# A four-layer hybrid encoder on one core: stacked gate logits, lower weight parts by adding DMAs, and other orders at three places

## The chip, the cores and the metric

The kernel runs on one core of a Trainium2 chip. The core has a matrix engine (TensorE, PE in the rows), a vector engine (DVE), an activation engine (ACT), a general engine (GpSimd, POOL) and a queue engine (SyncE, SP). Each works through its own instructions in order, and semaphores join them. The metric is the device time of one execution in microseconds (us).

## The reference, cut to what matters

Four layers work on 512 tokens of 1024 features: retention, a conformer convolution, gated linear attention (GLA) and retention again, each followed by an MLP with a squared ReLU. The GLA mixer makes a gate from a low-rank product, and normalises each head before a silu gate:

```
def log_gate(d):
    logits = (u @ gate_w1[d]) @ gate_w2[d] + gate_b[d]
    return split_heads(jax.nn.log_sigmoid(logits.astype(F32)) / GLA_GATE_NORMALIZER, GLA_HEADS)

o = bidirectional_scan(q, k, v, log_gate(0), log_gate(1))
o = merge_heads(rmsnorm(o, norm_gain)) * jax.nn.silu(r)
return o @ w_out
```

The gate's rank is 16. Retention rotates q and k by angles made of the positions, which needs a sine and a cosine of large arguments. The convolution has 31 taps over time for each feature, then a layer norm, a silu and a product.

## The kernel before

All activations lie with features on the partitions: a tile is 128 features by 512 tokens. Every fp32 product is made of three matmuls of rounded parts: high by high, low by high, high by low (`mm3`, lines 454 to 456). A weight panel is 128x1024. `Stream.prep` loads it into one of three raw buffers (`wraw`, a DMA on SP's queue), ACT copies it into the high part `whi` (line 146), and DVE subtracts to get the low part `wlo` (line 147). The ring holds six such pairs.

TensorE's order is the order in which the code is written. Norms and other side work are put into that order by `after(us, fn)`: the function runs when the matmuls written since then add up to so many us (`tick`). On ACT and DVE a scheduler orders the work by its own idea of time, except in blocks under `manual_schedule`, where the written order holds: the first norm (ACT, DVE), the convolution's taps and layer norm (ACT, DVE), and GLA (ACT). POOL is written by hand in layer 0.

The places that matter are these.

- The start. `first_norm` loads `h` and the first panels and splits `h` into `xh` and `xl`. `norm_sums` squares `h` on ACT (line 266) in halves of 256 tokens, and DVE adds the squares up (line 267). The mean of squares is a matmul (line 285), which `norm_at = 22.0` puts 22 us behind the start of the projections. `angles` (line 746) makes the sine and cosine: ACT rounds the angle to `ahi` (line 757), POOL takes off multiples of whole turns by five rounds of products (lines 772 to 779), DVE finishes (lines 762 to 789), ACT takes the sine, and `sr` and `cr` go out to HBM. DVE then rotates q and k (lines 865 to 867) and splits them into `qkh` and `qkl` (line 442). The first scores read those.
- The convolution. Tokens go in two halves, c0 and c1. `stats` takes mean and variance and the reciprocal root, with a load of ACT's table ahead of it (line 1192) and another behind it (line 1195). `finish` makes the silu (line 1206) and the split `zh`, `zl` of each of eight tiles. `second` (line 1235) runs `stats(c1)`, then tile 7 of c0, then the rest of c1.
- GLA. The gate's inner product leaves `u1`, split into `ogh` and `ogl`. `logits` makes eight `mm3` from it. For each head, `scores` copies a PSUM bank to `tmp` (line 1431), overwrites a block (line 1432), and splits it. `attend` makes the output, and `gate` a silu gate (lines 1525 and 1526). In the last head one gate lies ahead of `attend` and one behind it, and `fin` places the norm's mean.

In what follows, panel n of GLA is the one that lies n behind the stream's position (`W.at`) where the layer begins, as the diff counts them: panel 9 holds k's weights of head 1, panel 15 the second half of head 0's output weights.

Of the kernel before, what the change touches and what calls it, by code (L numbers as in the profile page):

```python
# [10 lines left out]
F32 = mybir.dt.float32  # L11
# [11 lines left out]
P = 128  # L23
# [5 lines left out]
HEADS = 4  # L29
CW = 31  # L30
PAD = CW // 2
TP = T + 2 * PAD
# [63 lines left out]
class Stream:  # L96


    def __init__(self, K, src, ahead):
        self.K, self.src, self.ahead = K, src, ahead  # L100
        self.n = src.shape[0]
        self.ready, self.loaded, self.at = [], 0, 0
        self.deep = 5
        self.aside = {}
        self.cut = {}
        self.pairs, self.steps = {}, []
        self.between = {}

# [4 lines left out]
    def prep(self, parts=1):  # L113

        if self.steps:
            self.steps.pop(0)()
            return []
        if self.loaded >= self.n:
            return []
        K = self.K  # L120
        nc = K.nc
        i = self.loaded
        if self.between.get(i):
            self.whole(self.between[i].pop(0), self.ring)
            return []
        if i in self.pairs:
            self.pair(i)
            return []
        self.loaded += 1
        if i in self.cut:  # L130
            self.whole(self.cut[i], self.aside.pop(i, self.ring))
            return []
        raw = K.wp.tile([P, 8 * P], F32, name="wraw", tag="wraw", bufs=3)
        hi, lo = self.aside.pop(i, self.ring)()
        pan = Panel(hi, lo)
        self.ready.append(pan)

        def load(a, b):
            nc.sync.dma_start(raw[:, a:b], self.src[i][:, a:b])

        def split(a, b):
            for c in range(a, b, min(pan.w, b - a)):
                d = c + min(pan.w, b - a)
                t, o = divmod(c, pan.w)
                h, l = (x[t][:, o:o + d - c] for x in (hi, lo))
                nc.scalar.activation(h, raw[:, c:d], AF.Copy)  # L146
                nc.vector.tensor_tensor(l, raw[:, c:d], h.bitcast(F32), ALU.subtract)  # L147

        if parts == 1:
            load(0, 8 * P)  # L150
            split(0, 8 * P)
        else:
            w = 8 * P // parts
            return [(lambda a=a: load(a, a + w), lambda a=a: split(a, a + w)) for a in range(0, 8 * P, w)]
# [188 lines left out]
class Kern:  # L343
# [166 lines left out]
    def norm_sums(self):  # L510

        self.hsum = Sums(self, D)
        for a, b in HALVES:
            for k in range(KD):
                self.hsum.add(self.h[k][:, a:b], (a, b))

    def norm(self, us, then):

        if self.hsum is None:
            self.norm_sums()  # L520
# [513 lines left out]
    def conv(self, layer, close):  # L1034
        nc = self.nc
        with self.tc.tile_pool(name="conv", bufs=1) as op:
            Z = [self.pair(op, "z", 2 * KD) for _ in range(KD)]
            with self.tc.tile_pool(name="taps", bufs=1) as cp:
# [148 lines left out]
                def stats(c):  # L1187
# [4 lines left out]
                    nc.scalar.preload_act_table_set("abs_reciprocal_sqrt_and_small")  # L1192
# [23 lines left out]
                with self.tc.manual_schedule(engines={ACT, DVE}):  # L1216
                    taps(c0)

                    def first():
                        complete(c0)  # L1220
                        stats(c0)
                        norm(c0)
                        finish(c0, 0, 1, 2, 3)
# [11 lines left out]
                    def second():  # L1235
                        stats(c1)
                        finish(c0, 7)
# [10 lines left out]
            with self.tc.tile_pool(name="outw", bufs=1) as wp:  # L1248
# [8 lines left out]
    def gla(self, layer, close):  # L1257
# [3 lines left out]
        with self.tc.tile_pool(name="gla", bufs=1) as gp:  # L1261
# [18 lines left out]

            u1 = self.pair(gp, "og", 8)
# [15 lines left out]
            def first(i, ps, c):  # L1297
                if i == 0:
                    t = self.tmp()
                    nc.vector.tensor_tensor(t[:, c[0]:c[1]], ps[:, c[0]:c[1]], self.r[:, c[0]:c[1]], ALU.mult)  # L1300
                    self.split(u1, t[:, c[0]:c[1]], c)
# [6 lines left out]

            def logits(p, h):
                for d in range(2):  # L1310
                    ps = self.ps()
                    self.mm3(ps, p.blk(d * HEADS + h), u1, True, True)
# [98 lines left out]
            def scores(h):  # L1411
# [7 lines left out]
                pr = []  # L1419
                for s in range(NB):  # L1420
# [12 lines left out]
                    p = self.pair(gp, "og", 8) if (h, s) == (0, 3) else self.pair(gp, "p" if s < 2 else "c23" if h + 1 == HEADS else "c01", 4)  # L1433
                    self.split(p, t)
                    pr.append(p)
# [29 lines left out]
            def attend(h, v, pr, g):  # L1465
# [22 lines left out]

                def finish():
                    self.rsqrt(ro, s2.mean((0, T)))  # L1490
                    if not g or h == 0:
                        for f in range(2):
                            normed(f)
                            if h == 0:
                                split(f)
# [3 lines left out]
                def rest():  # L1499
                    for f in range(len(g), 2):  # L1500
                        nc.vector.tensor_tensor(o[f], o[f], gate(), ALU.mult)
                        if not g:
                            split(f)
                    if h > 0 and g:
                        self.flush()
                        for f in range(2):
                            normed(f)
                            split(f)
# [39 lines left out]
            with self.tc.manual_schedule(engines={ACT}):  # L1548
                self.lead(3, first, tokens, 7.0)
                v = values(0)  # L1550
                p = self.W.next()
                logits(p, 0)
# [10 lines left out]
                for h in range(HEADS):  # L1563
# [16 lines left out]
                    if h > 0:  # L1580
                        g = [gate()] if last else []
                    rest = attend(h, v, pr, g)
# [13 lines left out]
    def run(self):  # L1596
        self.taps = [(0, 12), (8, 12), (8, 10), (8, 10), (8, 10), (16, 8), (24, 7), (16, 4)]
        self.shift_at = 40.0
        self.side = 6
        self.fin = 2.0, 7.0, 7.0, 2.0  # L1600
        self.ends = HALVES
        self.norm_at, self.tok_at = 22.0, 4.5
# [63 lines left out]
def _gla_panels(w_in, w1, w2, w_out):  # L1666
# [4 lines left out]
    for d in range(2):  # L1671
        w1p[:, 32 * d:32 * d + R] = w1[d]
        w2p[32 * d:32 * d + R, d] = w2[d]
# [84 lines left out]
```

## Time and profile before

| | us |
|---|---|
| three runs | 2712.33, 2715.22, 2720.29 |
| median | 2715.22 |
| the profiled execution | 2716.44 |
| its span in the trace | 2714.6 |
| TensorE busy | 2673.8 (98%) |
| DVE busy | 1934.6 (71%) |
| ACT busy | 1348.3 (50%) |
| POOL busy | 184.9 (7%) |

The engines' busy times add up to far more than the span because they overlap. TensorE's busy time lies 40.8 us under the span. The granted clock is shown for each window as a share of the full 2.4 GHz; a window that holds a stretch at 1.2 GHz shows a mean between 0.5 and 1. In a timeline a number in brackets is the time that the engine stood idle ahead of the instruction, with the instruction that released it.

### The profile page before, as it was taken

The page shows a single profiled execution, that of the slowest core. Times are in us where ns is not written, and L with a number is a line of the kernel's source. Part 1 is how long each engine was busy: PE and PEld are TensorE (multiplying, and loading weights), DVE is VectorE, ACT ScalarE, POOL GpSimd, SP SyncE. Part 2 cuts the span into 40 slices and gives each one's busy share as a digit, 9 for nine tenths or more (in the row PEclk, how much of TensorE's full clock was granted, in tenths as well). Part 3 has the DMA queues.
Part 4 walks back from the last instruction along what each step waited for, and adds up shares of the span by engine and source line. Part 5 has one row for each costly group of instructions (what it writes and reads, how often), then busy time and mean ns, then how long its engine had stood idle before and what let it go on. Part 6 is the DMA issues. An engine that isn't in the chain of part 4 may idle for free.

```text
span 2714.6 us, 38438 instructions
## 1 busy us (share of the span) xinstructions
PE 2673.8 (98%) x15238; PEld 2355.0 (87%) x15238; DVE 1934.6 (71%) x3016; ACT 1348.3 (50%) x2098; POOL 184.9 (7%) x207
## 2 busy tenths in 40 slices
PE   9999999999999999999999999999999999999998
PEld 7888889889998898999987888899888888989997
DVE  7755568877859977766788686677765555777766
ACT  5443444655536455554476555455544443555432
POOL 5420000000008400000000000000000000000000
PEclk9999999999999999999999999999999999999999
DMA  5433232776635422332222231333213222223322
GB/s 189 171 129 101 71 100 85 242 258 235 220 127 213 168 93 86 109 117 73 84 70 78 78 109 63 109 109 116 86 62 94 86 70 87 85 86 109 117 63 70
DMA packets 89028, 313.36 MB, mean 115 GB/s; under 512 B 9872, under 2 KB 12176, under 8 KB 88848
## 3 DMA queue, kind: packets, MB, share of 16 engines
q1 hardware_dynamic: 85536, 299.31, 33.4%
q0 software_dynamic: 3168, 11.54, 1.1%
q8 instruction: 119, 1.95, 0.3%
q14 instruction: 61, 0.50, 0.1%
q10 hardware_dynamic: 144, 0.07, 0.0%
HBM read 271.55 MB, written 39.32 MB: 115 GB/s over the span
## 4 chain that ended last, share of the span: by engine, by line
PE 82%; DVE 11%; ACT 3%; DMA 2%; POOL 1%; issue 1%; SPq 0%; DVEq 0%; ACTq 0%
PE ps L455 27%; PE ps L456 27%; PE ps L454 27%; DVE ps L1104 2%; DVE wlo L147 1%; DMA wraw<-in_wst_dram 1%; DMA cuth<-whi 1%; DVE acc L267 1%; ACT whi L146 1%; DVE tmp L329 1%; DMA cutl<-wlo 0%; DVE h L332 0%; PE st L275 0%; DVE actl L442 0%; DVE hc L1063 0%
## 5 line engine op out<-in xcount | busy, mean ns | idle before, releaser
L454 PE MATMUL ps<-xh,whi 128*128 128x256 f32 (+1 forms) x1920 | 644.0, 335 | 0.9 <-ACT xh L437 0.9
L455 PE MATMUL ps<-xl,whi 128*128 128x256 f32 (+1 forms) x1920 | 640.8, 334 | 1.1 <-DVE xl L444 1.1
L456 PE MATMUL ps<-xh,wlo 128*128 128x256 f32 (+1 forms) x1920 | 640.5, 334 | 0.0
L146 ACT ACTIVATE whi<-wraw 128x1024 fp32r<-128x1024 f32 (+1 forms) x300 | 312.2, 1045 | 317.5 <-PE ps L455 217.5
L147 DVE TENSOR_TENSOR wlo<-wraw,whi 128x1024 fp32r<-128x1024 f32 (+1 forms) x300 | 363.8, 1216 | 110.5 <-ACT whi L146 108.3
L455 PEld LDWEIGHTS ps<-xl,whi 128*128 128x128 f32 x1920 | 365.7, 190 | 38.7 <-DVE xl L444 1.5
L454 PEld LDWEIGHTS ps<-xh,whi 128*128 128x128 f32 x1920 | 365.9, 191 | 38.0 <-ACT xh L437 1.1
L456 PEld LDWEIGHTS ps<-xh,wlo 128*128 128x128 f32 x1920 | 365.8, 191 | 36.1 <-DVE wlo L147 0.5
L455 PE MATMUL ps<-actl,whi 128*128 128x512 f32 x896 | 350.1, 391 | 3.8 <-DVE actl L442 3.7
L454 PE MATMUL ps<-acth,whi 128*128 128x512 f32 x896 | 349.0, 390 | 0.6 <-ACT acth L435 0.6
L456 PE MATMUL ps<-acth,wlo 128*128 128x512 f32 x896 | 348.7, 389 | 0.0
L308 DVE TENSOR_TENSOR y<-y,ps 128x512 f32<-128x512 f32 (+1 forms) x200 | 114.8, 579 | 209.7 <-PE ps L456 209.0
L454 PE MATMUL ps<-wS,whi 128*128 128x256 f32 x768 | 217.7, 284 | 1.1 <-ACT tmp L654 1.1
L455 PE MATMUL ps<-wS,whi 128*128 128x256 f32 x768 | 217.3, 283 | 0.0
L456 PE MATMUL ps<-wS,wlo 128*128 128x256 f32 x768 | 217.3, 283 | 0.0
L455 PEld LDWEIGHTS ps<-actl,whi 128*128 128x128 f32 x896 | 168.2, 188 | 43.0 <-DVE actl L442 8.7
L454 PEld LDWEIGHTS ps<-acth,whi 128*128 128x128 f32 x896 | 168.2, 188 | 36.0 <-ACT acth L435 1.5
L456 PEld LDWEIGHTS ps<-acth,wlo 128*128 128x128 f32 x896 | 168.2, 188 | 34.6
L190 ACT ACTIVATE whi<-wraw 128x1024 fp32r<-128x1024 f32 x96 | 101.5, 1057 | 145.6 <-PE ps L455 114.8
L190 ACT ACTIVATE whi<-raw 128x1024 fp32r<-128x1024 f32 x96 | 81.2, 846 | 159.4 <-PE ps L455 126.3
L267 DVE TENSOR_TENSOR acc<-acc,sq 128x256 f32<-128x256 f32 (+1 forms) x246 | 121.3, 496 | 51.2 <-ACT sq L266 45.3
L454 PEld LDWEIGHTS ps<-wS,whi 128*128 128x128 f32 x768 | 147.4, 192 | 1.8 <-ACT tmp L654 1.7
(349 smaller groups left out, 5256.8 us busy)
## 6 DMA issues: line engine op xcount, KB each, us to landing
wraw<-in_wst_dram SPq DMA_DIRECT2D x390, 512.0 KB, 3.7
raw<-in_wst_dram SPq DMA_DIRECT2D x48, 512.0 KB, 4.2
cuth<-whi SPq DMA_DIRECT2D x24, 512.0 KB, 3.6
cutl<-wlo SPq DMA_DIRECT2D x24, 512.0 KB, 3.8
whi<-cuth SPq DMA_DIRECT2D x20, 512.0 KB, 3.3
wlo<-cutl SPq DMA_DIRECT2D x20, 512.0 KB, 4.3
diagh<-dg POOLq DMA_DIRECT2D x11, 512.0 KB, 3.2
diagl<-dg POOLq DMA_DIRECT2D x11, 512.0 KB, 3.2
```

What stands on the lines that cost most here:

```text
L146: nc.scalar.activation(h, raw[:, c:d], AF.Copy)
L147: nc.vector.tensor_tensor(l, raw[:, c:d], h.bitcast(F32), ALU.subtract)
L190: nc.scalar.activation(hi[0][:, :w], raw[:, :w], AF.Copy)
L267: nc.vector.tensor_tensor(acc, acc, t, ALU.add)
L308: self.K.nc.vector.tensor_tensor(y, y, ps[:, a:b], ALU.add)
L329: nc.vector.scalar_tensor_tensor(ts[k][:, a:b], self.ys[k][:, a:b], K.gain(self.layer, self.which, k), self.r[:, a:b], ALU.mult, ALU.mult)
L454: mm(out, lhsT=A[0], rhs=B[0], start=start, stop=False)
L455: mm(out, lhsT=A[0], rhs=B[1], start=False, stop=False)
L456: mm(out, lhsT=A[1], rhs=B[0], start=False, stop=stop)
L1104: nc.vector.scalar_tensor_tensor(sums[i], x, w, sums[i], ALU.mult, ALU.add)
```

## The change

Four parts of the code change.

1. The start. `norm_sums` takes its pieces as an argument, and the first norm (like the norms ahead of the convolution and GLA) squares 512 tokens at once, eight squares for sixteen. `norm_at` goes from 22 to 25.
2. The convolution. The load of ACT's root table leaves `stats`. In the first half it stands at the head of `first`, in the second half behind tile 7 of c0, which now goes ahead of `stats(c1)`. The block of the output weights keeps ACT's written order. Three taps of tile 7 go from DVE to ACT and POOL.
3. GLA's logits and weights. The rank-16 factors are packed three times at 32-row offsets (upper part, lower part, and upper part once more), so that one matmul on 96 rows makes what three did: 8 matmuls for 24. Only one low part of 32 rows is left to DVE, and `stack` copies 32 rows of the weight's low part on POOL. For eight panels (7, 9, ... 21) the low part is made otherwise: ACT writes the negative of the high part into `wlo`, and two DMAs on POOL's queue add the weights from HBM to it, 64 rows each (256 KB).
4. GLA's heads. `scores` issues the next copy of a bank ahead of the split of the one before. In the last head both gates come behind `attend`, and the norm's mean comes at 3.0 us for 2.0.

```diff
+                if i in self.adding:
+                    nc.scalar.activation(l, h.bitcast(F32), AF.Copy, scale=-1.0)
+                    for a in (0, P // 2):
+                        nc.gpsimd.dma_start(l[a:a + P // 2, :], self.src[i][a:a + P // 2, c:d], accum_op=ALU.add)
+                else:
+                    nc.vector.tensor_tensor(l, raw[:, c:d], h.bitcast(F32), ALU.subtract)
...
-    def norm_sums(self):
+    def norm_sums(self, pieces=HALVES):
...
-            self.norm_sums()
+            self.norm_sums(FULL)
...
                     nc.scalar.activation(var[:, a:b], mu[c][:, a:b], AF.Square)
-                    nc.scalar.preload_act_table_set("abs_reciprocal_sqrt_and_small")
...
                     def first():
+                        nc.scalar.preload_act_table_set("abs_reciprocal_sqrt_and_small")
                         complete(c0)
...
                     def second():
+                        finish(c0, 7)
+                        nc.scalar.preload_act_table_set("abs_reciprocal_sqrt_and_small")
                         stats(c1)
-                        finish(c0, 7)
...
-            with self.tc.tile_pool(name="outw", bufs=1) as wp:
+            with self.tc.tile_pool(name="outw", bufs=1) as wp, self.tc.manual_schedule(engines={ACT}):
...
+            self.W.adding = range(self.W.at + 7, self.W.at + 23, 2)
...
-                    self.split(u1, t[:, c[0]:c[1]], c)
+                    self.split_hi(u1, t[:, c[0]:c[1]], c)
+                    b = slice(GR, 2 * GR)
+                    u = u1[0][b, c[0]:c[1]]
+                    nc.vector.tensor_tensor(u, t[b, c[0]:c[1]], u.bitcast(F32), ALU.subtract)
...
+            def stack(p):
+                for hi, lo in zip(p.hi, p.lo):
+                    nc.gpsimd.tensor_copy(hi[2 * GR:3 * GR, :], lo[2 * GR:3 * GR, :].bitcast(F32))
...
-                    self.mm3(ps, p.blk(d * HEADS + h), u1, True, True)
+                    nc.tensor.matmul(ps, lhsT=p.blk(d * HEADS + h)[0], rhs=u1[0], start=True, stop=True)
+                    self.tick(0.2)
...
-                    p = self.pair(gp, "og", 8) if (h, s) == (0, 3) else self.pair(gp, "p" if s < 2 else "c23" if h + 1 == HEADS else "c01", 4)
-                    self.split(p, t)
-                    pr.append(p)
+                    held.append((s, t))
+                    if s > 0:
+                        parts(*held.pop(0))
+                parts(*held.pop(0))
...
                 def rest():
                     for f in range(len(g), 2):
+                        t = gate()
+                        assert done
+                        nc.vector.tensor_tensor(o[f], o[f], t, ALU.mult)
+                        split(f)
...
-                    if h > 0:
-                        g = [gate()] if last else []
-                    rest = attend(h, v, pr, g)
+                    rest = attend(h, v, pr, g if h == 0 else [])
...
-        self.taps = [(0, 12), (8, 12), (8, 10), (8, 10), (8, 10), (16, 8), (24, 7), (16, 4)]
+        self.taps = [(0, 12), (8, 12), (8, 10), (8, 10), (8, 10), (16, 8), (24, 7), (16, 7)]
...
-        self.fin = 2.0, 7.0, 7.0, 2.0
+        self.fin = 2.0, 7.0, 7.0, 3.0
-        self.norm_at, self.tok_at = 22.0, 4.5
+        self.norm_at, self.tok_at = 25.0, 4.5
```

The order on ACT shows three places. Line numbers of the changed kernel are higher by 8 at its front, by 26 at its end. At the start, before, ACT goes to the rounding of the angle (`ahi`) like this; `lge` is a small tile of the decay's logarithm, `sq<-h` a square for the norm:

```order
L909 ACTIVATE lge<-cst 128x8
L266 ACTIVATE sq<-h 128x256 x2
L910 ACTIVATE lge<-lge 128x8
L911 ACTIVATE lge<-lge 128x8
L146 ACTIVATE whi<-wraw 128x1024
L266 ACTIVATE sq<-h 128x256 x2
L146 ACTIVATE whi<-wraw 128x1024
L757 ACTIVATE ahi<-ang 128x512
L266 ACTIVATE sq<-h 128x256 x2
```

And in the changed kernel, where the first three rows of ACT are the branch, a DMA and the loads of two tables, `L505 ACT_TABLE_LOAD` and `L1227 ACT_TABLE_LOAD` (the line at the head of the convolution's `first`):

```order
L918 ACT_TABLE_LOAD
L918 ACTIVATE lge<-lge 128x8
L445 ACTIVATE xh<-h,cst 128x512
L148 ACTIVATE whi<-wraw 128x512
L919 ACT_TABLE_LOAD
L919 ACTIVATE lge<-lge 128x8
L148 ACTIVATE whi<-wraw 128x1024 x2
L443 ACTIVATE sq<-acc 128x512
L765 ACTIVATE ahi<-ang 128x512
```

Two loads of tables and the rounding of the squares' sum now stand ahead of `ahi`, and a third load stands ahead of `E` (line 929). In the convolution ACT passes from c0 to c1; before, with tile 7 of c0 as the last two rows:

```order
L1206 ACTIVATE y<-y,cst 128x256
L435 ACTIVATE zh<-y 128x256
L1191 ACTIVATE tmp<-ps 128x256
L1192 ACT_TABLE_LOAD
L461 ACTIVATE tmp<-tmp,eps 128x256
L1195 ACT_TABLE_LOAD
L1206 ACTIVATE y<-y,cst 128x256
L435 ACTIVATE zh<-y 128x256
```

In the changed kernel tile 7 is the first two rows here:

```order
L1213 ACTIVATE y<-y,cst 128x256
L443 ACTIVATE zh<-y 128x256
L1245 ACT_TABLE_LOAD
L1199 ACTIVATE tmp<-ps 128x256
L469 ACTIVATE tmp<-tmp,eps 128x256
L1202 ACT_TABLE_LOAD
L1213 ACTIVATE y<-y,cst 128x256
L443 ACTIVATE zh<-y 128x256
```

Tile 7 moved ahead of both loads; two copies of weights (`whi<-wraw`, line 146) that stood between the tiles of c0 moved behind tile 7 of c1 and four squares. In GLA, ACT comes to panel 9 behind the exponentials of head 0; before:

```order
L1371 ACTIVATE qs<-qs 128x384
L1372 ACTIVATE ks<-c 128x384
L146 ACTIVATE whi<-wraw 128x1024
L1519 ACT_TABLE_LOAD
L1519 ACTIVATE o<-o 128x512
L146 ACTIVATE whi<-wraw 128x1024
```

In the changed kernel:

```order
L1391 ACTIVATE qs<-qs 128x384
L1392 ACTIVATE ks<-c 128x384
L148 ACTIVATE whi<-wraw 128x1024
L151 ACTIVATE wlo<-whi 128x1024
L1545 ACT_TABLE_LOAD
L1545 ACTIVATE o<-o 128x512
```

The negative copy came in right behind the copy, DVE's subtraction of this panel is gone, and two adding DMAs on POOL stand between it and TensorE.

## Rows read from the trace of the kernel before

**Rows 1.** Windows of the span: busy time of each engine, granted clock (PEclk), DMA share, GB/s
```profile
0.00:50.00 50.00, 43.98 (x170) 35.40 (x171) 40.21 (x59) 29.87 (x53) 29.26 (x28) 0.93 0.60 199
50.00:100.00 50.00, 48.86 (x215) 40.08 (x215) 40.22 (x55) 21.67 (x28) 25.48 (x38) 1.00 0.49 169
900.00:950.00 50.00, 47.20 (x339) 44.87 (x337) 43.87 (x76) 22.87 (x37) 18.32 (x14) 0.97 0.44 156
950.00:1000.00 50.00, 47.52 (x367) 46.56 (x366) 36.09 (x83) 28.47 (x55) 0.00 (x0) 0.93 0.33 119
1400.00:1450.00 50.00, 47.73 (x264) 41.00 (x263) 41.11 (x81) 35.01 (x57) 0.00 (x0) 0.97 0.18 58
1550.00:1600.00 50.00, 46.56 (x315) 43.24 (x314) 39.48 (x81) 29.40 (x52) 0.00 (x0) 0.97 0.37 117
```

**Rows 2.** TensorE's waits: what waited for what, total us, times, longest
```profile
PE st L285 <- ACT sq L435: 3.3, 1, 3.3
PE ps L275 <- DVE acc L269: 2.7, 1, 2.7
PE ps L454 <- ACT zh L435: 2.4, 2, 1.4
PE ps L1422 <- DVE ogl L444: 2.3, 1, 2.3
PE ps L454 <- ACT ogh L435: 1.6, 1, 1.6
```

**Rows 3.** Timeline of ACT at the start: start us, us, engine line op out<-in, [idle before <-releaser]
```profile
20.55 0.62 ACT L757 ACTIVATE ahi<-ang 128x512 fp32r<-128x512 f32 x1
```

**Rows 4.** Timeline of POOL at the start: the first and the last step of one kind
```profile
22.14 3.08 POOL L773 TENSOR_SCALAR k<-k 128x512 f32<-128x512 f32 x1
...
48.81 0.62 POOL L773 TENSOR_SCALAR k<-k 128x512 f32<-128x512 f32 x1
```

**Rows 5.** Timeline of DVE round the end of POOL's chain
```profile
47.66 1.40 DVE L444 SCALAR_TENSOR_TENSOR vl<-ps,rcol,vh 128x512 fp32r<-128x512 f32 x2
52.81 0.43 DVE L762 TENSOR_SCALAR k<-acc 128x512 f32<-128x512 f32 x1 [3.74 <-POOL acc L777]
53.15 1.22 DVE L147 TENSOR_TENSOR wlo<-wraw,whi 128x1024 fp32r<-128x1024 f32 x1
```

**Rows 6.** Timeline of TensorE at the first scores
```profile
82.94 0.39 PE L454 MATMUL ps<-qkh 128*128 128x512 f32 x1
83.17 0.40 PE L455 MATMUL ps<-qkl,qkh 128*128 128x512 f32 x1
84.71 0.50 PE L456 MATMUL ps<-qkh,qkl 128*128 128x512 f32 x1 [1.14 <-DVE qkl L442]
```

**Rows 7.** Timeline of ACT in the convolution
```profile
939.95 1.06 ACT L146 ACTIVATE whi<-wraw 128x1024 fp32r<-128x1024 f32 x1 [1.96 <-PE ps L455]
...
951.71 1.28 ACT L1192 ACT_TABLE_LOAD   x1
953.01 0.51 ACT L461 ACTIVATE tmp<-tmp,eps 128x256 f32<-128x256 f32 x1
```

**Rows 8.** Timelines of ACT, DVE and TensorE at panel 9 of the linear attention
```profile
1393.60 1.05 ACT L146 ACTIVATE whi<-wraw 128x1024 fp32r<-128x1024 f32 x1
...
1396.46 1.22 DVE L147 TENSOR_TENSOR wlo<-wraw,whi 128x1024 fp32r<-128x1024 f32 x1
...
1397.74 0.50 PE L456 MATMUL ps<-xh,wlo 128*128 128x512 f32 x1
```

**Rows 9.** DMA issues of the page, and one such issue on POOL's timeline
```profile
diagh<-dg POOLq DMA_DIRECT2D x11, 512.0 KB, 3.2
...
55.96 0.77 POOL L1030 DMA_DIRECT2D diagh<-dg  x1 [0.31 <-POOL dg L1029]
```

**Rows 10.** Timeline of TensorE at panel 15
```profile
1457.08 0.50 PE L456 MATMUL ps<-ogh,wlo 128*128 128x512 f32 x1 [0.95 <-DVE wlo L147]
```

**Rows 11.** Timeline of TensorE at the end of the linear attention
```profile
1570.07 0.39 PE L455 MATMUL ps<-ogl,whi 128*128 128x256 f32 x1 [0.91 <-DVE ogl L442]
```

More of the change, by code (lines that the diff above doesn't have):

```diff
@@ L31 @@
 PAD = CW // 2
+GR = 32
 TP = T + 2 * PAD
@@ L107, in __init__ @@
         self.between = {}
+        self.adding = ()
     def ring(self):
@@ L146, in split @@
                 nc.scalar.activation(h, raw[:, c:d], AF.Copy)
-                nc.vector.tensor_tensor(l, raw[:, c:d], h.bitcast(F32), ALU.subtract)
+                if i in self.adding:
[4 more added lines that the diff above has]
+                    nc.vector.tensor_tensor(l, raw[:, c:d], h.bitcast(F32), ALU.subtract)
         if parts == 1:
@@ L508, in first_norm @@
         nc.sync.dma_start(self.cst[:, g:], self.cst_src[:, g:])
-    def norm_sums(self):
+    def norm_sums(self, pieces=HALVES):
         self.hsum = Sums(self, D)
-        for a, b in HALVES:
+        for a, b in pieces:
             for k in range(KD):
@@ L1419, in scores, with parts @@
                 pr = []
+                def parts(s, t):
+                    p = self.pair(gp, "og", 8) if (h, s) == (0, 3) else self.pair(gp, "p" if s < 2 else "c23" if h + 1 == HEADS else "c01", 4)
+                    self.split(p, t)
+                    pr.append(p)
+                held = []
                 for s in range(NB):
@@ L1487, in split @@
                     self.split(og[f], o[f])
+                done = []
                 def finish():
                     self.rsqrt(ro, s2.mean((0, T)))
[L1491 to L1495, printed above, removed]
+                    for f in range(2):
+                        normed(f)
+                        if h == 0:
+                            split(f)
+                    done.append(h)
                 self.after(self.fin[h], finish)
@@ L1500, in rest @@
                     for f in range(len(g), 2):
[L1501 to L1508, printed above, removed]
+                        t = gate()
+                        assert done
+                        nc.vector.tensor_tensor(o[f], o[f], t, ALU.mult)
+                        split(f)
                     return og
@@ L1551, in gla @@
                 p = self.W.next()
+                stack(p)
                 logits(p, 0)
@@ L1670, in _gla_panels @@
     R = w1.shape[2]
-    for d in range(2):
-        w1p[:, 32 * d:32 * d + R] = w1[d]
-        w2p[32 * d:32 * d + R, d] = w2[d]
+    for a in (0, GR, 2 * GR):
+        for d in range(2):
+            o = a + GR // 2 * d
+            w1p[:, o:o + R] = w1[d]
+            w2p[o:o + R, d] = w2[d]
     q = lambda h: _feat(w_in, h)
```

## The prediction

> **What bounds the kernel now.** TensorE is busy 98% of the span, so the time is its work, what it waits, and what it loses at the lower clock. I read the windows first: the granted clock is 0.93 or 0.97 in five of the stretches shown, and there a part of the window ran at 1.2 GHz instead of 2.4 [rows 1]. A mean of 0.93 over 50 us is a loss of 0.07 x 50 = 3.5 us, 0.97 is 1.5 us. Then I read TensorE's own waits: 3.3 us at the first norm's mean, 2.7 at the convolution's mean, 2.4 at the tiles `zh`, 2.3 and 1.6 in GLA [rows 2]. Each of these waits lies in a window with a lowered clock. The wait of 1.14 us for `qkl` at 84.71 lies in one at full clock [rows 1, 6]. I take it from this that a wait costs itself and, if it is long, another 1.5 to 3.5 us. The change aims at exactly these places, so the question is for each: does the wait vanish, or does the next late thing take it over? Last I read the engines' timelines at each place.
>
> **The start: +6.7 us, from -1 to +10.** The mean moves 15 matmuls later. A matmul of 512 columns follows the last one in 0.23 us [rows 6], so TensorE reaches the mean 3.4 us later, and the wait of 3.3 us goes, its clock loss of 3.5 with it. But these 6.8 us only bring TensorE sooner to the first scores, where it waits for `qkl` even now, until 84.71 [rows 6]. What ends last at the scores is another chain: ACT rounds `ahi` at 20.55 [rows 3], POOL runs its range reduction from there without a pause, and DVE, which idled 3.74 us for it, begins at 52.81 and works almost without a gap to `qkl` [rows 5, 6]. So the stage moves with that chain alone, and the gain of 6.8 is zero here. The change touches the chain in three places.
> First, ACT. The root table's load that stands at the head of `first` depends on nothing, and the order shows it as ACT's second table load in the whole program. It throws out the table of logarithms loaded just ahead of it, so two loads stand ahead of `ahi`; a load takes 1.28 us [rows 7], together 2.6. Eight squares of double width for sixteen I take as even. The rounding of the sum, of the same size as `ahi` (0.62) [rows 3], also went ahead of it. `ahi` comes 3.2 us later.
> Second, POOL. The same step takes 3.08 us beside DVE's sums of squares and 0.62 later on [rows 4]. With fewer, larger sums DVE disturbs POOL less: I take -1.0, bounded by 0 and by -2.5 (that one row's excess).
> Third, DVE behind POOL. The order puts one more panel's subtraction (1.22), two splits of `vl` (1.40 for both) and one product of a gate (0.6, about half a `vl` pair) behind the wait for POOL [rows 5]: 3.0 us, from 1 to 4, as the first may fill gaps in which DVE waits for the sine's transfer. The write of the cosine also stands one weight load later on SP's queue; I add nothing for it, up to 1.4.
> The chain's sum is 3.2 - 1.0 + 3.0 = +5.2. TensorE then waits some 12 us in pieces at the scores (5.2 + 6.8), which will cost clock: I take the smaller price, 1.5, from 0 to 3.5. With both it is +6.7.
> The Trainium skill, "ScalarE: Activation LUTs", section on what ACT_TABLE_LOAD costs, counts about 1.38 us of draining beside the load's 1.28. The trace doesn't show it behind the load: the load of 951.71 is followed at 953.01 by the next instruction [rows 7]. By the page the two loads would cost 5.3 us instead of 2.6, and the start +9.4.
>
> **The convolution: -6.5 us, from -8.5 to -3.** At c0 three DVE taps less of tile 7 (512 columns each, like a `vl` split 0.7 us [rows 5], now on ACT and POOL) bring the mean about 0.9 us sooner; that is bounded, since its sums wait for the same tile's matmuls in either kernel. At c1 tile 7 of c0 stood behind two table loads, 951.71 and the one following, and TensorE waited for its `zh` [rows 2, 7]; now it goes ahead of both. The two weight copies inside c0's tiles (939.95 is one, with a wait of 1.96 us for a matmul ahead of it) [rows 7] move behind, so c0's tiles end sooner too. The stretch's waits of 2.4 and its clock loss of 3.5 make 5.9; I take 5.6 of it and 0.9 at the mean. What may come late instead are the weight copies: ACT now makes them behind c1's tiles, and the MLP's first sums of squares behind those, a wait of 0 to 1.5 us. I take 0, since the MLP needs these panels only later.
>
> **GLA, front half: +2 us, from -4 to +8.** Sixteen matmuls of 512 less save 16 x 0.23 = 3.7 us; DVE must empty their banks, and I take 2.3. Then comes panel 9. ACT's copy ended at 1394.65, DVE's subtraction at 1397.68, and TensorE took the result at 1397.74 [rows 8]: just in time. In the changed kernel the negative copy takes another 1.05, to 1395.7. POOL then issues two transfers, 0.77 each. A queue of POOL's moves 512 KB in 3.2 us from issue to landing [rows 9]. No adding transfer is in this trace. I take 3.2 for each, since half the bytes should offset a read of the destination; it could be 2 or 8. The second lands at 1395.7 + 0.77 + 3.2 = 1399.7. TensorE, 2.3 us early, would be there at 1395.4: a wait of 4.3, with 1.5 of clock. That is +5.8. Part returns: at 1425 TensorE waits 2.3 us for `ogl` with a clock loss of 1.5 [rows 1, 2], an engine chain of ACT and DVE that the removed subtractions and the earlier bank copies shorten: -3.8. Panel 15 is late already, 0.95 us [rows 10]; with 1.5 to 2.5 us more for the adding way it costs about +2.3 with some clock. The sum is -2.3 + 5.8 - 3.8 + 2.3 = +2.0. The other six panels are copied well ahead of their use, and I price them at 0.
> The Trainium skill, "DMA: Bandwidth & Descriptors", anatomy of one DMA, gives 2.0 us and bytes over 436 GB/s for a transfer of GpSimd's queue. That agrees with the row at 512 KB, and makes 2.6 us for 256 KB, an estimate; it doesn't say whether adding takes longer. By it the front half would be near +1.
>
> **GLA, end: -4 us, from -4.5 to -2.** The last head's split waits on a gate whose silu comes late: waits of 1.6 and 0.9 us and 1.5 of clock [rows 1, 2, 11], together 4.0. Now both gates come behind `attend`, with 24 matmuls (5.5 us) as cover for the norm, and the first split is ready before TensorE is. The second is a close call.
>
> **The sum.** +6.7 - 6.5 + 2.0 - 4.0 = -1.8 us on the profiled execution's 2716.44, or 2714.6. The median of the runs is 1.2 us under that execution, so I say 2713.4. Less than 0.3% (8.1 us) is about what a measurement of this kernel can't tell from no change.
>
> **Rivals.** (a) Faster: the adding transfers land within 2 us, DVE's release is worth its full price, and the start's chain grows by 2 us at most. Then the start is +2, the convolution -7.4, GLA -4 and -4.4: -13.8, or 2701.5. For it speaks that each removed wait carries its clock loss. Against it speak the two table loads, which stand in the order.
> (b) Slower: the adding transfers. They take as long as an issue, a read of HBM and an addition together. Each us beyond 3.2 adds a us at panel 9 and one at panel 15, and far beyond that at the other six too. A landing of 8 us gives 2 x 4.8 = +9.6 and two more clock losses, 3: 2713.4 + 12.6 = 2726. It becomes slower than 8.1 us at some 7.5 us of landing, or at 6 if the start costs 10. For it speaks that a transfer must read what it adds to. Against it speaks the light load of the DMA engines there, a share of 0.18 [rows 1].
> (c) The change doesn't do what it says at one place: the table's load should go out of the way of c0's statistics, and goes to the program's start; ACT loads it anew at the old place. I hold this for nearly certain from the order, and it is in the forecast, worth +2.6 at the start; if the load stood where it is written, the time would be 2710.8.
>
> **Chances.** The forecast (within 0.3%, own range 2707 to 2721) 0.46; faster by (a) or parts of it 0.29; slower by (b), or by the start at its upper bound, 0.25. For 8 in 10 the range takes in most of (a) and (b): 2702 to 2725.
>
> **What would show it.** In the changed kernel's trace TensorE should not wait at the first mean, should wait some 12 us before about 91 us, for `qkl`, with ACT's `ahi` near 23.5. The wait at c1's first tile should be gone and the clock full there. A new wait on panel 9, 4 us for `wlo` released by a DMA, is the sharpest sign; if none is there, (a) holds in GLA. If the first scores start at 85 or sooner, my chain at the start is wrong.

## The result

The changed kernel takes 2731.4 us (median; 2730.08 to 2734.34), the kernel before 2714.34 in the same comparison: a ratio of 1.0063, interval 1.0051 to 1.0076. It is slower by 17 us, where I said 2713.4 and a range of 2702 to 2725. Its profiled span is 2729.3 us against 2714.6.

TensorE's waits of the changed kernel, in the columns of [rows 2]:

```profile
PE ps L464 <- DMA wlo<-in_wst_dram: 19.3, 2, 11.2
PE st L283 <- DVE acc L275: 3.3, 3, 1.6
...
PE ps L462 <- ACT qkh L443: 2.7, 2, 1.8
PE ps L464 <- DVE qkl L450: 2.4, 2, 2.0
PE st L827 <- DVE rx L477: 2.1, 1, 2.1
...
PE ps L462 <- ACT zh L443: 1.0, 1, 1.0
...
PE ps L462 <- ACT ogh L443: 0.7, 1, 0.7
```

The old waits are gone or small: none is left for the first mean, `zh` fell from 2.4 to 1.0, `ogh` from 1.6 to 0.7. Their place is taken by `rx` (the root that DVE makes of the mean), `qkh` and `qkl` at the start, and above all by two waits, 19.3 us together, for low parts that a DMA brings. The windows say where, as in [rows 1]:

```profile
50.00:100.00 50.00, 44.90 (x181) 35.41 (x180) 40.55 (x55) 19.44 (x24) 28.61 (x40) 0.90 0.48 169
...
900.00:950.00 50.00, 49.01 (x357) 46.35 (x356) 44.45 (x78) 26.35 (x44) 25.24 (x19) 1.00 0.46 171
950.00:1000.00 50.00, 47.15 (x384) 46.29 (x383) 39.12 (x85) 29.76 (x54) 0.00 (x0) 1.00 0.36 125
1350.00:1400.00 50.00, 41.59 (x250) 36.68 (x249) 43.04 (x80) 37.23 (x55) 4.71 (x5) 0.93 0.34 92
1400.00:1450.00 50.00, 45.76 (x249) 39.16 (x249) 34.39 (x71) 30.06 (x51) 3.28 (x4) 0.90 0.28 67
1450.00:1500.00 50.00, 41.48 (x213) 35.03 (x214) 26.36 (x49) 36.36 (x53) 5.38 (x7) 0.90 0.42 99
```

The convolution runs at full clock now (1.00 twice). The clock falls instead behind the first scores (0.90) and in GLA (0.93, 0.90, 0.90). Panel 9 on POOL's timeline and TensorE's:

```profile
1392.95 0.81 POOL L153 DMA_DIRECT2D wlo<-in_wst_dram  x1 [19.81 <-ACT wlo L151]
1397.64 0.80 POOL L153 DMA_DIRECT2D wlo<-in_wst_dram  x1 [3.89 <-issue]
...
1403.92 0.77 PE L464 MATMUL ps<-xh,wlo 128*128 128x512 f32 x1 [11.19 <-DMA wlo<-in_wst_dram]
```

The second adding DMA is issued 3.89 us after the first issue has ended, with nothing shown to wait for, and TensorE waits 11.19 us. This answers [rows 8], where the same product started at 1397.74 without a wait.

To see where time goes, I took the same matmul in two traces and subtracted its starts. The lag behind the kernel before, in us, at matmuls that stand in the trace of before at the times in the head row:

| kernel | 100 | 925 | 970 | 1010 | 1340 | 1397 | 1400 | 1500 | 1610 | 2700 |
|---|---|---|---|---|---|---|---|---|---|---|
| changed | +4.7 | +3.2 | -4.9 | -2.6 | -2.9 | -5.0 | +8.2 | +14.4 | +15.0 | +14.6 |
| e1_no_adding | +6.6 | +5.9 | -2.2 | +0.3 | +0.4 | -2.3 | -0.6 | -4.9 | -5.7 | -6.0 |
| e2_adding_alone | +0.8 | -1.2 | -2.6 | -2.6 | -2.7 | -2.6 | +8.2 | +16.6 | +16.4 | +15.7 |
| e3_skip_9_15 | +5.9 | +4.2 | -3.8 | -1.5 | -1.3 | -4.3 | -1.4 | -0.1 | -1.2 | -1.3 |
| e6_ring448 | +5.6 | +3.6 | -4.5 | -2.1 | -2.1 | -5.1 | +3.4 | +7.5 | +6.6 | +6.2 |
| e7_start_undone | -1.1 | -2.7 | -10.8 | -8.5 | -8.4 | -10.3 | -7.4 | -10.9 | -10.3 | -10.6 |
| e8_no_first_load | +5.5 | +3.5 | -4.5 | -2.2 | -2.1 | -4.0 | -2.6 | -6.8 | -7.8 | -7.9 |
| e9_gates_undone | +1.5 | +0.2 | -7.9 | -5.5 | -5.6 | -7.5 | -3.9 | -8.1 | -4.8 | -5.0 |
| e11_halves_at25 | +4.0 | +2.2 | -5.8 | -3.5 | -3.0 | -3.9 | -2.9 | -7.1 | -6.5 | -7.0 |
| e13_first_halves | -0.7 | -1.5 | -9.5 | -7.2 | -6.6 | -9.3 | -7.6 | -11.8 | -12.7 | -13.2 |
| e5_plain_copy | +5.3 | +4.2 | -3.9 | -1.6 | -0.8 | -3.7 | +3.6 | +5.0 | +5.6 | +4.9 |
| e10_six_room | +6.2 | +5.1 | -2.9 | -0.5 | -0.4 | -3.4 | -0.3 | -4.1 | -3.4 | -4.2 |
| e12_one_dma_room | +6.6 | +7.7 | -0.4 | +1.9 | +2.1 | 0.0 | +7.4 | +9.8 | +10.4 | +10.2 |

Each row is one execution. The kernels e7 and e9 have the same start and differ by 2.6 us at 100; the seven traces with the whole changed start (changed, e1, e3, e5, e6, e10, e12) lie between 4.7 and 6.6. So a step of less than some 2.5 us in one row proves little by itself.

### The profile page after: what moved, and what is told of

It is laid out like the page before. It is cut to its first block, busy times and chain, and to the rows that moved or that the text cites. A ratio compares the mean times of both kernels' runs of the same rounds, so it can differ in the third digit from the quotient of the medians.

```text
span 2729.3 us, 38412 instructions
## 1 busy us (share of the span) xinstructions
PE 2672.5 (98%) x15222; PEld 2352.1 (86%) x15222; DVE 1923.2 (70%) x2984; ACT 1362.3 (50%) x2090; POOL 204.1 (7%) x227
## 4 chain that ended last, share of the span: by engine, by line
PE 82%; DVE 10%; ACT 3%; DMA 2%; issue 1%; POOL 1%; SPq 0%; DVEq 0%; ACTq 0%; POOLq 0%
PE ps L463 27%; PE ps L464 27%; PE ps L462 27%; DVE ps L1112 2%; DMA wraw<-in_wst_dram 1%; DVE wlo L155 1%; ACT whi L148 1%; DVE acc L275 1%; DVE tmp L337 1%; DVE h L340 0%; DMA cuth<-whi 0%; PE st L283 0%; DMA wlo<-in_wst_dram 0%; DVE tmp L1061 0%; DVE actl L450 0%
## 5 line engine op out<-in xcount | busy, mean ns | idle before, releaser
L464 PE MATMUL ps<-xh,wlo 128*128 128x256 f32 (+1 forms) x1920 | 640.7, 334 | 11.2 <-DMA wlo<-in_wst_dram 11.2
L155 DVE TENSOR_TENSOR wlo<-wraw,whi 128x1024 fp32r<-128x1024 f32 (+1 forms) x292 | 353.9, 1215 | 117.7 <-ACT whi L148 115.0
L462 PEld LDWEIGHTS ps<-acth,whi 128*128 128x128 f32 x896 | 168.2, 188 | 35.6 <-ACT acth L443 0.6
```

The lines of the kernel that those rows point to most:

```text
L462: mm(out, lhsT=A[0], rhs=B[0], start=start, stop=False)
L464: mm(out, lhsT=A[1], rhs=B[0], start=False, stop=stop)
```

## The experiments

### Is the adding way the loss?

e1_no_adding:

```diff
-            self.W.adding = range(self.W.at + 7, self.W.at + 23, 2)
+            self.W.adding = ()
```

> The changed kernel with no panel made by adding; everything else of the change stays. Theory A (the two waits for adding DMAs at panels 9 and 15, 11.4 and 8.3 us in the trace, with their clock loss, are the whole loss): both go, and 14 to 22 us come back, so 2710 to 2717. Rival B (the start, with three more table loads and its later scores, and the end of GLA are the loss; the waits on adding DMAs only absorb what is late anyway): DVE's subtractions come back late and TensorE waits for them, so 2724 or more.

Measured: 2708.63 us, ratio 0.9983 (0.9974 to 0.9992) to the kernel before. Theory A holds and rival B falls: 22.8 us come back, somewhat more than the 14 to 22 expected. What is left of the change is a small gain of 0.17%. At panel 9 a wait remains, for DVE:

```profile
PE ps L464 <- DVE wlo L155: 1.7, 1, 1.7
```

e2_adding_alone is the kernel before with this alone:

```diff
+                if i in self.adding:
+                    nc.scalar.activation(l, h.bitcast(F32), AF.Copy, scale=-1.0)
+                    for a in (0, P // 2):
+                        nc.gpsimd.dma_start(l[a:a + P // 2, :], self.src[i][a:a + P // 2, c:d], accum_op=ALU.add)
...
+            self.W.adding = range(self.W.at + 7, self.W.at + 23, 2)
```

> The kernel before with the adding way for the same eight panels and nothing else of the change. Theory A: slower than the kernel before by 14 to 20 us, so 2728 to 2735, with waits of some 9 and 7 us for wlo at panels 9 and 15. Rival B (the adding way hurts only because the stacked logits bring TensorE to panel 9 five us sooner): at most +8, so 2723 or less.

Measured: 2731.91 us, ratio 1.0066 (1.0049 to 1.0082). The adding way alone costs what the whole change costs, without the stacked logits and the other orders:

```profile
PE ps L463 <- DMA wlo<-in_wst_dram: 9.5, 1, 9.5
PE ps L463 <- ACT tmp L1339: 8.9, 1, 8.9
```

The first row is panel 15, the second panel 9: there the profile puts the wait down to an ACT instruction that had long been done, and the wait ends where the panel's second adding DMA lands. Rival B, which allowed at most 8 us, falls.

e3_skip_9_15:

```diff
-            self.W.adding = range(self.W.at + 7, self.W.at + 23, 2)
+            self.W.adding = [self.W.at + n for n in (7, 11, 13, 17, 19, 21)]
```

> The changed kernel with six panels by adding (7, 11, 13, 17, 19, 21) instead of eight; 9 and 15 go by DVE again. Theory A: no wait of TensorE for an adding DMA is left, and 14 to 22 us come back: 2710 to 2717. Rival C (adding costs at every panel, by POOL's queue, the DMA engines or SBUF): the loss falls in proportion, by a quarter, so 2725 or more.

Measured: 2716.66 us, ratio 1.0006 (0.9997 to 1.0016). Two of eight panels carry most of the loss, so C falls. But 8 us above e1 is not nothing; a wait of 2.7 us for an adding DMA is left, so theory A's "no wait" is missed, with a short stretch at the lower clock behind it. It is at panel 17, the second gate panel of head 1: TensorE has just done panel 16, and the wait ends where the fourth of the six pairs of DMAs lands. In the table it is part of the rise from -1.4 at 1400 to -0.1 at 1500 (-4.7 at 1460):

```profile
PE ps L464 <- DMA wlo<-in_wst_dram: 2.7, 1, 2.7
```

### Why does an adding DMA take so long?

e6_ring448:

```diff
-    nc = bacc.Bacc("TRN2", target_bir_lowering=False, num_devices=1, dynamic_dma_scratch_size=256)
+    nc = bacc.Bacc("TRN2", target_bir_lowering=False, num_devices=1, dynamic_dma_scratch_size=448)
```

> The changed kernel with room for 448 instead of 256 bytes of descriptors for POOL's DMAs, nothing else. In the changed kernel's trace each adding DMA is issued 0.3 us after the one before it has landed, though the program has no wait between them. Theory D (two adding DMAs don't fit into the room for descriptors, so the second waits until the first is done): the pause of 3.9 us between the two issues of a panel goes below 0.5, panels 9 and 15 come some 4 us sooner, and 6 to 9 us come back: 2722 to 2726. Rival E (an adding DMA holds POOL until it has landed, whatever the room): the pause stays at 3.9 us and the time at 2731 within 2.

Measured: 2724.74 us, ratio 1.0038 (1.0023 to 1.0053). Theory D holds, E falls: POOL issues both DMAs of panel 9 back to back, in 1.63 us, and 6.7 us of the 17 come back. Panel 9's wait falls from 11.2 to 6.7 us, as D has it; panel 15's only from 8.1 to 6.4: its second DMA, now in flight beside the first, takes 6.9 us to land where it took 4.3. POOL's timeline, the chain that ended last, and the DMA issues of 1360 to 1520 (KB each, median us to landing):

```profile
1393.04 1.63 POOL L153 DMA_DIRECT2D wlo<-in_wst_dram  x2 [23.55 <-ACT wlo L151]
...
1393.58 5.58 DMA wlo<-in_wst_dram
...
wlo<-in_wst_dram POOLq DMA_DIRECT2D x16, 256.0 KB, 6.3
```

The landing is now 6.3 us where the changed kernel has 4.3 for each of two in a row:

```profile
wlo<-in_wst_dram POOLq DMA_DIRECT2D x16, 256.0 KB, 4.3
```

TensorE's waits of e6 at panels 9 and 15; the second is again put down to an instruction that had long been done:

```profile
PE ps L464 <- DMA wlo<-in_wst_dram: 6.7, 1, 6.7
PE ps L464 <- ACT whi L148: 6.4, 1, 6.4
```

e5_plain_copy takes the addition away:

```diff
-nc.gpsimd.dma_start(l[a:a + P // 2, :], self.src[i][a:a + P // 2, c:d], accum_op=ALU.add)
+nc.gpsimd.dma_start(l[a:a + P // 2, :], self.src[i][a:a + P // 2, c:d])
```

> The changed kernel with the sixteen DMAs of POOL's queue plain, without the addition (the low parts are then the weights themselves, so that the subtraction is left out). Theory L (the addition is what fills the room for descriptors and takes the time): the pause between the two issues of a panel goes, as does most of the 4.4 us of landing (to 2.5 us or less), and the time falls to 2716 to 2722. Rival M (any DMA of 64 rows on POOL's queue behaves so): pause and time as in the changed kernel, 2731.

Measured, in one execution: 2721.47 us, in theory L's range. The pause is gone at the old room of 256 bytes, so rival M falls: the addition fills the room, and plain DMAs of the same size don't. What of the addition fills it stays open. But theory L fails in its second half: a plain DMA takes 5.0 us to land, not 2.5.

```profile
1394.39 1.05 POOL L153 DMA_DIRECT2D wlo<-in_wst_dram  x2 [24.22 <-ACT wlo L151]
...
wlo<-in_wst_dram POOLq DMA_DIRECT2D x16, 256.0 KB, 5.0
```

So the addition itself adds 1.3 us to a landing (6.3 against 5.0 us with both in flight). What costs more is the path as a whole, a copy, an issue and a transfer one behind another, and the wait for room.

e12_one_dma_room has the 448 bytes and one DMA of 128 rows:

```diff
-                    for a in (0, P // 2):
-                        nc.gpsimd.dma_start(l[a:a + P // 2, :], self.src[i][a:a + P // 2, c:d], accum_op=ALU.add)
+                    nc.gpsimd.dma_start(l, self.src[i][:, c:d], accum_op=ALU.add)
```

> The changed kernel with 448 bytes of room and one adding DMA of 128 rows for each panel instead of two of 64. If the transfer's bytes set the landing, it lands as late as the second of two (some 6 us from the issue) and the time is that of the run with room, 2723 to 2726. If a fixed cost for each DMA sets it, it lands 1 us or more sooner: 2720 to 2722.

Measured, in one execution: 2726.55 us. The DMA lands in 5.6 us instead of 6.3, TensorE's waits at panels 9 and 15 are 5.4 and 4.5 us instead of 6.7 and 6.4. The time is near the first case (bytes set the landing). But this execution was 4 us behind e6 before GLA began, so the time decides nothing; from 1340 to 1500 it loses 7.7 us where e6 loses 9.6, which leans to a part saved for each DMA.

```profile
wlo<-in_wst_dram POOLq DMA_DIRECT2D x8, 512.0 KB, 5.6
PE ps L463 <- DMA wlo<-in_wst_dram: 9.9, 2, 5.4
```

e10_six_room joins e3 and e6: six panels, 448 bytes.

> Six panels by adding (not 9 and 15), with 448 bytes of room for descriptors instead of 256. Without room this was 2716.7, with one wait of 2.7 us for an adding DMA at panel 13 and its clock loss; without any adding it was 2708.6. Theory N (an adding DMA that lands in time gains nothing and costs nothing, since DVE isn't what ends last at these six panels): the wait goes, 2707 to 2711. Rival O (the eight ACT copies less six for DVE's subtractions are worth something where they are in time): below 2706. Rival P (adding keeps a cost at each panel): 2713 or more.

Measured: 2711.47 us, ratio 0.9990 (0.9981 to 1.0000). No wait for an adding DMA is left, and 5 us of e3's come back. (The wait that went is the one at panel 17, which the expectation puts at panel 13.) The time is 0.5 us above what theory N gave; O falls. The interval takes in N and the lower end of P, and overlaps that of e1, which has no adding: a price of up to some 3 us for the six panels isn't excluded. Adding in time gains nothing, and no cost of it is clear.

### What is the start worth?

e7_start_undone is e1 with the first part of the change undone, for all norms, and without the load at the head of `first`:

```diff
-            self.norm_sums(FULL)
+            self.norm_sums()
...
-                        nc.scalar.preload_act_table_set("abs_reciprocal_sqrt_and_small")
                         complete(c0)
...
-        self.norm_at, self.tok_at = 25.0, 4.5
+        self.norm_at, self.tok_at = 22.0, 4.5
```

> The changed kernel without adding, and with its first part undone: the first norm in halves at 22 us, and no load of the root table at the head of the convolution's first half. Without adding alone it was 2708.6, with the first scores 6.6 us later than in the kernel before. Theory F (the start's part of the change is a pure loss of 5 to 7 us, since the chain over ahi, POOL and DVE sets the end of this stage and not the mean): 2701 to 2704, first scores within 1 us of the kernel before. Rival G (the first scores' delay is one that later stages absorb): 2707 to 2709.

Measured: 2705.79 us, ratio 0.9974 (0.9965 to 0.9984). It lies between F and G. The table has both: the start is 7.7 us shorter than in e1, as F has it, and GLA takes some of it back (from 1340 to 1610 e1 gains 6.1, this one 1.9).

e8_no_first_load is e1 with this:

```diff
                     def first():
-                        nc.scalar.preload_act_table_set("abs_reciprocal_sqrt_and_small")
                         complete(c0)
```

> The changed kernel without adding and without the load of the root table at the head of the convolution's first half; the norm's new pieces and place stay. Three table loads of the start go. Theory H (the loads are the cause of the start's loss): ahi 2.6 us sooner than in the changed kernel and the first scores with it, 2705 to 2706. Rival I (POOL takes the 2.6 us back, as it did in the changed kernel, where ahi came 2.2 us later and POOL's chain ended at the same 52.7; the loss is DVE's work behind POOL): 2708 to 2709.

Measured: 2707.85 us, ratio 0.9977 (0.9968 to 0.9987), against e1 a difference of 0.8 that the intervals don't separate. The trace decides for I: ACT has `ahi` 1.8 us sooner than in the changed kernel, and POOL's chain still ends at the same place. The changed kernel first, then this one:

```profile
22.70 0.62 ACT L765 ACTIVATE ahi<-ang 128x512 fp32r<-128x512 f32 x1
52.78 0.43 DVE L770 TENSOR_SCALAR k<-acc 128x512 f32<-128x512 f32 x1 [7.19 <-POOL acc L785]
```

```profile
20.89 0.62 ACT L765 ACTIVATE ahi<-ang 128x512 fp32r<-128x512 f32 x1
52.79 0.43 DVE L770 TENSOR_SCALAR k<-acc 128x512 f32<-128x512 f32 x1 [8.64 <-POOL acc L785]
```

DVE starts at 52.8 in both, and in the kernel before at 52.81 [rows 5]. An earlier `ahi` buys nothing here; which part of DVE's work slows POOL's steps by as much isn't settled. It isn't the size of the sums of squares: this kernel has the whole squares, and its POOL chain, begun early, takes as long as that of the kernels with halves (see the last section).

e11_halves_at25 is e8 with the squares in halves again, and the mean still at 25:

```diff
-            self.norm_sums(FULL)
+            self.norm_sums()
```

> The changed kernel without adding and without the first table load, the first norm's squares again in halves, but its mean still at 25 us. The order on DVE behind POOL is then that of the changed kernel, with the vl splits, one more weight subtraction and one gate product ahead of qkl. Theory Q (the place of the mean, through the order on DVE behind POOL's chain, is the start's loss): as without the first load alone, 2707 to 2709, first scores some 5 us later than in the kernel before. Rival R (the squares of 512, which load ACT more in its first cycles, are the loss): as with the start undone, 2705 to 2706.5, first scores within 2 us.

Measured: 2709.86 us, ratio 0.9985 (0.9976 to 0.9994), with the first scores 4.0 us late. That is theory Q (though 0.9 us above its range) and not R. From e7 it differs in the place of the mean alone; the intervals of the two overlap, so it is the traces that separate them. e7 first, then this one, TensorE's last wait at the scores:

```profile
83.60 0.50 PE L464 MATMUL ps<-qkh,qkl 128*128 128x512 f32 x1 [1.19 <-DVE qkl L450]
```

```profile
52.24 0.43 DVE L770 TENSOR_SCALAR k<-acc 128x512 f32<-128x512 f32 x1 [5.91 <-POOL acc L785]
87.25 0.80 PE L464 MATMUL ps<-qkh,qkl 128*128 128x512 f32 x1 [0.46 <-DVE qkl L450]
```

DVE starts behind POOL at 51.93 and 52.24, almost together, and the last `qkl` comes 3.7 us later. From DVE's start behind POOL to the end of the fourth `qkl` it takes 31.6 to 32.1 us in the five traces with the mean at 22 (before, e2, e7, e9, e13), and 34.0 to 35.6 us in the nine with the mean at 25. In those nine one more `wlo` and two `vl` lie in between. So the place of the mean is the start's loss, by what it moves behind POOL on DVE.

e13_first_halves is e7 with the first norm as before, and the norms ahead of the convolution and of GLA as changed:

```diff
-            self.norm_sums()
+            self.norm_sums(HALVES if us == self.norm_at else FULL)
```

> As the run with the start undone (2705.8, ratio 0.9974), but only the first norm's squares stay in halves; the norms ahead of the convolution and of GLA keep whole squares, as in the change. In the trace of the run with the start undone, GLA's front half gave back 3 us of the 7.7 that the start had won. Theory S (the halves ahead of GLA are what gave it back, by the waits at its norm and at panel 9): 2702 to 2704. Rival T (TensorE comes sooner and the chains of DVE and ACT there don't, whatever the squares): 2705 to 2707.

Measured: 2704.38 us, ratio 0.9962 (0.9948 to 0.9975). It falls between S and T and its interval overlaps that of e7; the table leans to S (from 1340 to 1610 it gains 6.1, as e1). This kernel is faster than both kernels of the case; against the one before, by 0.25% to 0.52%.

### What is the end of GLA worth?

e9_gates_undone is e7 with `finish` and `rest` as in the kernel before, and:

```diff
-                    rest = attend(h, v, pr, g if h == 0 else [])
+                    if h > 0:
+                        g = [gate()] if last else []
+                    rest = attend(h, v, pr, g)
...
-        self.fin = 2.0, 7.0, 7.0, 3.0
+        self.fin = 2.0, 7.0, 7.0, 2.0
```

> As the run with the start undone, and the last head's gates put back to one ahead of attend and one behind, with the norm's mean at 2.0. Theory J (the end of GLA was worth the 4 us that the prediction priced): 4 us slower than the run with the start undone, 2705 to 2708. Rival K (the splits still wait behind the new order, so it is worth 1 us, as the trace of the changed kernel has it): at most 1.5 us slower, 2702 to 2704.5.

Measured: 2707.64 us, ratio 0.9976 (0.9966 to 0.9985). The 1.9 us to e7 lie within the intervals. In the trace the old order loses 3.3 us from 1500 to 1610, e7 loses 0.6: the new order is worth 2.7 where TensorE comes there 8 to 11 us sooner than in the kernel before. That trace is of an execution 4.1 us above the median of e9, so the 2.7 may be too much. The time lies in J's range, but J counted from 2701 to 2704 for e7, which took 2705.79; by the difference neither J (4) nor K (1.5 at most) is hit.

```profile
1563.33 0.58 PE L462 MATMUL ps<-ogh,whi 128*128 128x256 f32 x1 [4.30 <-ACT ogh L443]
```

This wait was 1.6 in the kernel before [rows 2]: it has grown with TensorE's lead. TensorE came there 8.1 us sooner, and `ogh` only 5.4.

## Why the prediction was wrong, step by step

- **The start: the path right, the sum near by luck.** Forecast +6.7, in the changed kernel's trace +4.7. As forecast, the wait at the first mean brought nothing when it went, and the last `qkl` ends the stage. But all four terms were off. `ahi` came 2.2 us later, not 3.2. POOL gave back all of it, not 1.0. DVE's work behind POOL added 2.2, where I had 3.0. The lower clock cost 2.5, where I had 1.5:

```profile
86.88 0.79 PE L464 MATMUL ps<-qkh,qkl 128*128 128x512 f32 x1 [0.46 <-DVE qkl L450]
...
91.31 0.63 PE L462 MATMUL ps<-qkh 128*128 128x512 f32 x1
91.74 0.63 PE L463 MATMUL ps<-qkl,qkh 128*128 128x512 f32 x1
```

This answers the wait at 84.71 of [rows 6]; at 91 the matmuls still follow one another in 0.43 us, where it is 0.23 in [rows 6], so the clock is still the lower one. Two of the causes fail with their terms. The table loads, which I blamed for 2.6, are worth next to nothing (e8): POOL takes the delay back. And POOL takes it back because it starts later, not because the sums of squares are fewer and larger: in e8 they are as large, `ahi` comes at 20.89, and POOL's chain takes as long as with halves (last section). What is left is the order on DVE behind POOL (e11).

- **The signs at the start.** `ahi` came at 22.70 for 23.5, and no wait is left at the first mean. But the waits at the scores make 5.1 us, not some 12, and end at 86.88: TensorE came there only 3.4 us sooner than before, not 6.8, as it now waits 2.1 us for `rx` behind the mean. The first score starts at 80.79 (before, 82.25), so by my own last sign the chain is wrong. It still ends the stage, but of its three parts only DVE's made it longer.

- **The convolution: the sum near, again by misses that offset each other.** Forecast -6.5, measured -5.8 (from 925 to 1010). The mean gave 3.7 (from +3.2 at 925 to -0.5 at 950), where I had 0.9, and tile 7 gave 4.4 (to -4.9 at 970), where I had 5.6. I had put the late weight copies and sums at 0 of a bound of 1.5, and they cost 2.3: two of the three waits for `acc` at L283 in the result's list are theirs, 0.98 us at 983.86 and 0.79 at 999.73. (The third, of 1.6, is at the end of the kernel, before as after.)

- **GLA's front half: here the prediction failed.** Forecast +2.0, measured +17.3 (from 1340 to 1500). The logits (-2.1, forecast -2.3) and the wait at 1425 (from +8.9 at 1420 to +5.1 at 1430, -3.8 as forecast) were right in size. For that wait the cause isn't shown: it goes in e1, without the adding way, but as well in e2, without the earlier bank copies, where TensorE simply comes 8 us later. Panel 9 cost 13.2 where I had 5.8 (the table, 1397 to 1400), panel 15 8.7 where I had 2.3 (from +5.7 at 1450 to +14.4 at 1460). The step that fell is the landing: "the second lands at 1395.7 + 0.77 + 3.2". From the end of the negative copy at 1392.59 it took not 4.0 but 11.2 us: 0.4 to the issue, 4.7 to the second issue, 6.1 to land. I had named the landing as the point from which rival (b) decides, and the rival's outcome came; but its cause as I put it, that reading what is added to takes long, is not the one: the addition adds 1.3 us to a landing (e5). The issues follow one another only when the one before has landed, for want of room (e6), and a plain transfer on this path is slow as well (e5). I had priced the issue from a row of a queue's plain DMAs, one at a time, and never asked what two in a row do.

- **GLA's end: wrong.** Forecast -4.0, measured +0.6. Of the waits of 1.6 and 0.9 the first shrank to 0.7 and the second stayed, at 1.0, with a short stretch at the lower clock behind them; and the MLP's first products wait twice, 0.8 and 0.9 us, where one wait of 0.9 stood. With no adding (e1) the end gave -0.8. I had taken it that the first split would be ready before TensorE; it wasn't. What holds it up, the norm or the gate, wasn't tried apart.

- **Sum and chances.** The trace is 16.4 us off the sum (+14.6 against -1.8). The two panels account for 13.8, as (13.2 - 5.8) + (8.7 - 2.3), and the end of GLA for 4.6; the start gave 2.0 back. My bound let issue and landing grow to some 9 us behind the negative copy, and they took 11. Put into rival (b)'s formula, the 11.2 us are a landing of 10.4 and give 2730.8, close to the 2731.4 measured, but in part by luck: the panels cost 13.8 of the 17.4 that it adds, and the rest came from GLA's end. One slip in (b): with its two clock losses the limit of 8.1 us is reached at a landing of some 6.7 us, not 7.5.

## What to carry to other kernels

Before a subtraction is moved from an engine to a chain of copy, issue and transfer, ask how long before its use the operand is ready; two panels without that lead cost more than eight could gain. Price the second of two transfers, not the first: what they share (here the room for descriptors on POOL's queue) serialises them, and nothing in a list of waits says so. A removed wait is worth what the next late chain leaves of it: find that chain first, and then ask what the edit does to its order.

## What the hardware showed that I had not expected

- With 256 bytes of room for descriptors, an adding DMA of 64 rows of 4 KB on POOL's queue is issued only 0.3 us after the one before has landed: the issues stood 4.69 us apart (1392.95 and 1397.64), of another panel the same (1404.09, 1408.68). With 448 bytes they followed at once. Plain DMAs of the same shape followed at once with 256.

```profile
1404.09 0.82 POOL L153 DMA_DIRECT2D wlo<-in_wst_dram  x1 [5.65 <-ACT tmp L1352]
1408.68 0.82 POOL L153 DMA_DIRECT2D wlo<-in_wst_dram  x1 [3.77 <-issue]
```

- From HBM into SBUF POOL's queue took, in the median, 4.3 us for 256 KB alone with an addition (3.7 to 6.1 in the changed kernel), 6.3 with two in flight, 5.0 plain with two in flight, 5.6 for 512 KB in one. The Trainium skill, "DMA: Bandwidth & Descriptors", anatomy of one DMA, gives 2.0 us and the bytes over 436 GB/s for such a DMA, by which I estimate 2.6 us for 256 KB and 3.2 for 512. The transfers from SBUF to HBM in [rows 9] agree with it, those of these runs don't. The direction alone isn't the reason: SP's queue loads panels of 512 KB from HBM in 3.6 us, in the same stretch of the changed kernel. Such loads were under way during most of these DMAs, three of them during the 6.1 us of panel 9's second; what they cost it wasn't tried.

```profile
wraw<-in_wst_dram SPq DMA_DIRECT2D x19, 512.0 KB, 3.6
```

- POOL's range reduction takes less time the later it starts. In e7 it starts at 20.73 and DVE takes over at 51.93, in e1 at 23.74 and 53.17: of 3.0 us of delay 1.2 are left at its end. e7 has the squares in halves, e1 whole; but e8, with whole squares and an early start, takes 31.2 us like e7 and not 29.4 like e1, and its first step takes 2.93 us. What in DVE's work does this wasn't tried.

```profile
20.73 0.64 POOL L780 TENSOR_SCALAR k<-ahi 128x512 f32<-128x512 f32 x1 [17.98 <-ACT ahi L765]
51.93 0.43 DVE L770 TENSOR_SCALAR k<-acc 128x512 f32<-128x512 f32 x1 [4.42 <-POOL acc L785]
```

```profile
23.74 0.80 POOL L780 TENSOR_SCALAR k<-ahi 128x512 f32<-128x512 f32 x1 [20.99 <-ACT ahi L765]
53.17 0.43 DVE L770 TENSOR_SCALAR k<-acc 128x512 f32<-128x512 f32 x1 [6.92 <-POOL acc L785]
```

```profile
21.60 2.93 POOL L780 TENSOR_SCALAR k<-ahi 128x512 f32<-128x512 f32 x1 [18.84 <-ACT ahi L765]
```
